# Two K^T tiles, 512-column products in three projections, and a new tile layout in a two-layer diffusion block on one core

## The chip, the cores and the metric

The kernel runs on one core of a Trainium2 chip. The metric is the device time of one execution in microseconds (us). TensorE (PE) multiplies, with its weight loads listed as PEld; VectorE is DVE, ScalarE is ACT, GpSimd is POOL and SyncE is SP. SP and POOL issue the transfers.

## The reference, cut to what matters

Two layers act on 256 tokens of width 2048; only layer 0 also carries 256 context tokens. All matrices are float32.

```python
# layer 0: gated delta rule (16 heads of 128) beside a gated short convolution
p = h @ w_in                      # for x and for ctx
q, k, v = split(silu(conv(qkv)))  # q, k normalised
o, S = _gdn_chunk_scan(f(qc), f(kc), f(vc), ...)   # context first, both directions
o, _ = _gdn_chunk_scan(f(qx), f(kx), f(vx), ..., s_ctx)
y_b = b_g * conv(c_g * h_b, w_conv_b) * silu(z_b)
x = x + gate * (concat([rmsnorm(o) * silu(z), y_b]) @ w_out)
# layer 1
u, v = split(gelu(uv))
y_c = u * (w_s @ layernorm(v) + b_s) * silu(z_c)
y_d = einsum(mean_of_neighbours(p_d) - p_d, pool_w) * pool_scale * silu(z_d)
x = x + gate * (concat([y_c, y_d]) @ w_out)
return rmsnorm(x, final_norm_w)
```

## The kernel before

Float32 accuracy comes from splitting: every weight chunk of 128x1024 values (512 KB) is loaded (`raw`), rounded to a high part `H` on ACT (line 202), and the rest `L` is formed on DVE (line 209); `wchunk` does this, with four buffers each for raw, H and L, and `extra` pools that add a buffer to every third chunk in two places. Activations are split the same way. A product is then the sum of three: H with the activation's high part, H with its low part, and L with its high part. Each product instruction loads 128x128 weights of its own.

The work stands in this order:

- The first keys and values (`wset`): for each of 16 slices of the model width, modulation, normalised transposed activations (`h_cols`, into `hxH`, `hxL`, `hcH`, `hcL`, x and context), and products of six blocks of 128 (`k_part`, line 450) that are added up in six `acc` tiles in SBUF.
- The other keys and values (`proj` on `wkv`, 10 steps; products at line 230), each 2 blocks of 128 for 256 tokens of x and 256 of context. Key rows go to memory (`ktd`, `kkd`, `vvd`) and come back by head group. The gates of the delta rule are made by `ab_rows` in step 6.
- The delta rule in four groups of four heads. A group loads K^T (`KTt`), K and V on POOL's queue, projects the queries (`wq`) and the gate (`wza`), forms Gram matrices (`G`) and masks, inverts triangular blocks (`LB`, `PT`, `XT`, `X`), and then scans eight steps (`kS`, `QS`, `z`, `Sp`, `az`), ending in a norm (`on`) and a transpose (`oT`). Between these the scheduler puts products of `wq`, `wza` and `wbb` (short convolution), 24 blocks of 192 products each.
- The output projection of layer 0, the norm and split of `h1`, and layer 1: value (`wv1`), pool branch (`wpz`, `poolw`), token mix (`wuz`), output (`wout1`).

A scheduler that simulates the program sets the order on every engine before it runs; the order is then fixed. PSUM tiles `pj` (two banks of 512 columns each) exist twice, so a projection can start only when the one before the last has been read out.

The output projections (`projT_n`) take the weights chunk as the moving side, 512 columns at a time. `proj` takes the activations as the moving side, 256 columns at a time:

```python
for i, (w, t) in enumerate(((wH, 0), (wH, 1), (wL, 0))):
    for e, a in enumerate(acts):
        PE.matmul(o[:, e * 256:(e + 1) * 256] if m > 1 else o, w, a[t][:, k, :], ...)
```

Of the kernel before, what the change touches and what calls it, by code (L numbers as in the profile page):

```python
# [17 lines left out]
P = 128  # L18
# [52 lines left out]
def layout(a):  # L71
# [44 lines left out]
    r["poolw"] = f(a["o_pool_w"][0].reshape(4, 4, P, 512).transpose(0, 2, 1, 3)).reshape(4, P, D)  # L116
# [6 lines left out]
def body(ctx: ExitStack, tc: tile.TileContext, T, dbg=None):  # L123
# [187 lines left out]
    hx_stack = ExitStack()  # L311
    hxp = pool("hx", stack=hx_stack, side="right")
    hxH = hxp.tile([P, KT, 256], F32R, name="hxH")
    hxL = hxp.tile([P, KT, 256], F32R, name="hxL")
# [50 lines left out]
    with ExitStack() as ph1:  # L365
        hcp = pool("hc", stack=ph1)
        hcH = hcp.tile([P, KT, 256], F32R, name="hcH")
        hcL = hcp.tile([P, KT, 256], F32R, name="hcL")

        accp = pool("acc", stack=ph1)  # L370
        with ExitStack() as ph0:
# [6 lines left out]
            acc = [accp.tile([P, 2, 512], F32, name="kacc", tag=f"kacc{b}") for b in range(6)]  # L378
# [39 lines left out]
            def norm_tok(s):  # L418
                for n in (2 * s, 2 * s + 1):
                    junk = accp.tile([P, 2, 512], F32, name="junk", tag="kacc5")  # L420
# [9 lines left out]
            def h_cols(j, srcs=(0, 1)):  # L430
                tr = gp.tile([P, 4, P], F32, name="trp", tag="g")
                for s in srcs:
                    aH, aL = ((hxH, hxL), (hcH, hcL))[s]
# [10 lines left out]
            def k_part(w, j, ps, first, last, srcs):  # L444
                for n in range(6):
                    wH, wL = (t[:, n * P:(n + 1) * P] for t in w)
                    for i, (w_, t) in enumerate(((wH, 0), (wH, 1), (wL, 0))):
                        for q in srcs:
                            a = ((hxH, hxL), (hcH, hcL))[q]
                            PE.matmul(ps[n][:, q * 256:(q + 1) * 256], w_, a[t][:, j, :],  # L450
                                      start=first and i == 0 and q == 0, stop=last and i == 2, skip_group_check=True)
# [33 lines left out]
            if "hT" in dbg:  # L485
                tap("hT", hcH.bitcast(F32))
# [4 lines left out]
        def row(name):  # L491
            return ap.tile([64, 512], F32, name=name)

        def ab_proj():
                nonlocal ab
                wab = ap.tile([P, KT, 64], F32, name="wab")
# [4 lines left out]
                for k in range(KT):  # L501
                    for t in range(2):
                        for e, a in enumerate(((hxH, hxL), (hcH, hcL))):
                            PE.matmul(abp[:, 256 * e:256 * e + 256], wHL[:, k, :], a[t][:, k, :],
                                      start=k == 0 and t == 0 and e == 0, stop=k == KT - 1 and t == 1,
                                      skip_group_check=True)
# [112 lines left out]
        for step, b in enumerate((12, 13, 2, 3, 6, 7, 10, 11, 14, 15)):  # L619
# [3 lines left out]
            proj(T["wkv"][b // 4, b // 2 % 2, b % 2], 256, [(hxH, hxL), (hcH, hcL)], [ps[:, 0, :], ps[:, 1, :]], 1)  # L623
# [3 lines left out]
            if step == 6:  # L627
                ab_rows()

# [43 lines left out]

    tick[0], tick[2] = RATE[1], 1
    y_stack = ExitStack()
    with ExitStack() as ph2:
# [6 lines left out]
        for grp in range(4):  # L683
            h0 = grp * 4
            hs = slice(h0, h0 + 4)
            KTt = A.tile([P, 4, 512], F32, name="KTt", tag="KTt")
# [14 lines left out]
            proj(T["wq"][grp], 512, [(hxH, hxL)], [ps[:, n, :] for n in range(4)], 2)  # L701
# [503 lines left out]
```

## Time and profile before

| | |
|---|---|
| median of 3 runs | 2149.61 us (2144.79 to 2152.18) |
| the profiled execution | 2155.28 us, its span 2153.5 us |
| PE, PEld busy | 96%, 90% |
| DVE, ACT busy | 71%, 46% |
| data moved | 446 MB, mean 207 GB/s |

A product is pipelined: it lasts 0.28 us (256 columns) but the next one starts about 0.12 us after it. So a busy share near 100% only says that PE has no gap, and the pace is read from starts: the time from the first start to the last of a run of equal instructions, divided by the steps between them.

### The profile page before, as it was taken

To read this page: it belongs to the slowest core of one execution; us is meant where nothing else is said; L and a number is where in the kernel's file an instruction comes from. 1 tells how busy PE (TensorE), PEld (TensorE's weight loads), DVE (VectorE), ACT (ScalarE), POOL (GpSimd) and SP (SyncE) were. 2 spreads that over 40 slices of the span, in tenths; PEclk is the share of its full clock that TensorE was granted. 3 is DMA by queue.
4 is the path that set the end of the run, shared out by engine and by line. 5 is a ranking of instruction groups with operands and counts; after the bars stand their busy time and mean duration, and the time that the engine had idled before them with its cause. 6 is when DMAs were issued, how large, how long until landed. Compare 5 with 4: busy or idle time off the path is not lost. (4 is left out here: it accounts for less than half of the span.)

```text
span 2153.5 us, 42176 instructions
## 1 busy us (share of the span) xinstructions
PE 2069.5 (96%) x17034; PEld 1928.5 (90%) x17034; DVE 1526.0 (71%) x2715; ACT 999.5 (46%) x1728; POOL 33.8 (2%) x51
## 2 busy tenths in 40 slices
PE   6999999999999999989999999898999999999997
PEld 4789999999989999989999878677899999998886
DVE  4447987877976898489758984788687676555554
ACT  5333365225554546445645554345454444444433
POOL 0000000000000000000000000000000000000000
PEclk9999999999999999999999999999999999999999
DMA  9777655776544775366448862797866666666664
GB/s 343 263 262 243 188 182 174 238 247 233 179 134 139 247 258 179 91 225 195 133 139 258 276 187 79 253 326 260 275 219 189 180 186 197 195 187 215 192 194 131
DMA packets 151267, 446.41 MB, mean 207 GB/s; under 512 B 16512, under 2 KB 23456, under 8 KB 150048
## 3 DMA queue, kind: packets, MB, share of 16 engines
q1 hardware_dynamic: 145936, 425.37, 61.8%
q0 software_dynamic: 5136, 18.35, 2.7%
q8 instruction: 133, 2.18, 0.4%
q14 instruction: 62, 0.51, 0.1%
HBM read 423.19 MB, written 20.46 MB: 206 GB/s over the span
## 5 line engine op out<-in xcount | busy, mean ns | idle before, releaser
L209 DVE TENSOR_TENSOR L<-raw,H 128x1024 fp32r<-128x1024 f32 (+1 forms) x554 | 667.6, 1208 | 374.8 <-ACT H L202 354.1
L202 ACT CAST H<-raw 128x1024 fp32r<-128x1024 f32 (+1 forms) x554 | 574.4, 1042 | 761.7 <-PE pj L230 419.4
L230 PE MATMUL pj<-hxH,H 128*128 128x256 f32 x1856 | 528.5, 285 | 4.2 <-DVE zb L946 4.2
L230 PE MATMUL pj<-hxH,L 128*128 128x256 f32 x1856 | 527.3, 284 | 0.0
L230 PE MATMUL pj<-hxL,H 128*128 128x256 f32 x1856 | 526.8, 284 | 0.0
L230 PEld LDWEIGHTS pj<-hxH,H 128*128 128x128 f32 x1856 | 352.4, 190 | 6.3 <-DVE zb L946 4.5
L230 PEld LDWEIGHTS pj<-hxH,L 128*128 128x128 f32 x1856 | 352.4, 190 | 2.4 <-issue 1.2
L230 PEld LDWEIGHTS pj<-hxL,H 128*128 128x128 f32 x1856 | 352.4, 190 | 1.0
L230 PE MATMUL pj<-h1H,H 128*128 128x256 f32 x1024 | 290.5, 284 | 0.0
L230 PE MATMUL pj<-h1H,L 128*128 128x256 f32 x1024 | 289.8, 283 | 0.0
L230 PE MATMUL pj<-h1L,H 128*128 128x256 f32 x1024 | 289.7, 283 | 0.0
L277 DVE SCALAR_TENSOR_TENSOR acc<-araw,cs,acc 128x512 f32<-128x512 f32 x240 | 178.9, 747 | 33.0 <-DMA araw<-in_ada 20.8
L230 PEld LDWEIGHTS pj<-h1H,H 128*128 128x128 f32 x1024 | 196.5, 192 | 0.2 <-issue 0.2
L230 PEld LDWEIGHTS pj<-h1L,H 128*128 128x128 f32 x1024 | 196.5, 192 | 0.0
L230 PEld LDWEIGHTS pj<-h1H,L 128*128 128x128 f32 x1024 | 196.5, 192 | 0.0
L230 PE MATMUL pj<-hcH,L 128*128 128x256 f32 x320 | 90.4, 283 | 0.0
L230 PE MATMUL pj<-hcH,H 128*128 128x256 f32 x320 | 90.4, 282 | 0.0
L230 PE MATMUL pj<-hcL,H 128*128 128x256 f32 x320 | 90.1, 281 | 0.0
L239 PE MATMUL pj<-H,y1H 128*128 128x512 f32 x192 | 76.0, 396 | 0.0
L241 PE MATMUL pj<-H,y1L 128*128 128x512 f32 x192 | 75.9, 396 | 0.0
L240 PE MATMUL pj<-L,y1H 128*128 128x512 f32 x192 | 75.9, 395 | 0.0
L230 PEld LDWEIGHTS pj<-hcH,L 128*128 128x128 f32 x320 | 60.1, 188 | 0.5 <-issue 0.4
(428 smaller groups left out, 3659.6 us busy)
## 6 DMA issues: line engine op xcount, KB each, us to landing
raw<-in_wbb SPq DMA_DIRECT2D x128, 512.0 KB, 3.8
raw<-in_wout SPq DMA_DIRECT2D x128, 512.0 KB, 4.0
araw<-in_ada SPq DMA_DIRECT2D x192, 256.0 KB, 4.5
raw<-in_ada SPq DMA_DIRECT2D x64, 512.0 KB, 6.5
raw<-in_wpz SPq DMA_DIRECT2D x64, 512.0 KB, 3.9
raw<-in_wuz SPq DMA_DIRECT2D x64, 512.0 KB, 3.6
raw<-in_wkv SPq DMA_DIRECT2D x40, 512.0 KB, 4.7
araw<-in_ada0g SPq DMA_DIRECT2D x64, 256.0 KB, 4.5
```

The lines of the kernel that those rows point to most:

```text
L202: S.copy(H, raw)
L209: V.tensor_tensor(L, raw, H, ALU.subtract)
L230: PE.matmul(o[:, e * 256:(e + 1) * 256] if m > 1 else o, w, a[t][:, k, :], start=st and i == 0 and e == 0, stop=sp and i == 2, skip_group_ ...
L239: PE.matmul(o, xH[:, t], H[:, kk, :], start=st, stop=False, skip_group_check=True)
L240: PE.matmul(o, xH[:, t], L[:, kk, :], start=False, stop=False, skip_group_check=True)
L241: PE.matmul(o, xL[:, t], H[:, kk, :], start=False, stop=sp, skip_group_check=True)
L277: V.scalar_tensor_tensor(aacc[u // KT], raw, cs[:, k, 0:1], aacc[u // KT], ALU.mult, ALU.add)
```

## The change

- x and context activations move into one tile `hxc`, ordered (source, part, slice, token). `proj` for keys and values, `k_part` and the gate projection multiply both sources in one 512-column product, in place of two of 256 columns.
- `hx` for the delta rule is a copy of the x half, made by ACT (eight copies of 128x1024) in steps 7 to 9, in a slot that `acc8` (the `acc` tiles, the gate weights `wab` and two rows of `ab_rows`) held before.
- In layer 1, `pair` takes the place of `proj` for `wpz`, `poolw` and `wuz`: one 512-column product of H with both parts of the activation side by side, and one 256-column product of L with the high part. The halves that belong together are in different PSUM columns: ACT copies one out and DVE adds the other (`join`, or the first operation of the pool branch). A `pair` is 2 blocks of 128 and fills a `pj` tile.
- `KTt` comes from a pool of two tiles. `yb2` and `part` reuse the slots of `hx` and `KTt`.
- The `extra` pools `xh`, `xl` go, and `dynamic_dma_scratch_size` is 2048 in place of 4096.

```diff
-        hcp = pool("hc", stack=ph1)
-        hcH = hcp.tile([P, KT, 256], F32R, name="hcH")
-        hcL = hcp.tile([P, KT, 256], F32R, name="hcL")
+        hxcp = pool("hxc", stack=ph1, side="right")
+        hxc = hxcp.tile([P, 2, 2, KT, 256], F32R, name="hxc")
...
+    def both(t, k):
+        return hxc[:, :, t, k, :]
...
-                        for e, a in enumerate(acts):
-                            PE.matmul(o[:, e * 256:(e + 1) * 256] if m > 1 else o, w, a[t][:, k, :],
-                                      start=st and i == 0 and e == 0, stop=sp and i == 2, skip_group_check=True)
+                        PE.matmul(o, w, acts(t, k),
+                                  start=st and i == 0, stop=sp and i == 2, skip_group_check=True)
...
-                wab = ap.tile([P, KT, 64], F32, name="wab")
+                wab = acc8[:, 6].rearrange("p a b -> p (a b)").rearrange("p (k c) -> p k c", k=KT)
...
             if step == 6:
                 ab_rows()
+                hx = hxp.tile([P, 2, KT, 256], F32R, name="hx", tag="hx")
+            if step > 6:
+                for t in range(2):
+                    for q in range(1 if step < 9 else 2):
+                        k4 = slice(4 * (step - 7 + q), 4 * (step - 6 + q))
+                        S.copy(hx[:, t, k4], hxc[:, 0, t, k4])
...
+    KTp = pool("ktp", 2, stack=y_stack, side="right")
...
-            KTt = A.tile([P, 4, 512], F32, name="KTt", tag="KTt")
+            KTt = KTp.tile([P, 4, 512], F32, name="KTt", tag="KTt")
...
-        xh, xl = pool("xh", 1, stack=ph3), pool("xl", 1, stack=ph3)
-        extra[0] = [(None, None, None), (None, None, None), (None, xh, xl)]
...
+    def pair(src, x, kts=KT):
+        ps = pj.tile([P, 2, 2, 256], F32, name="pj", tag="pj")
+        for c in range(kts // 4):
+            H, L = wchunk(src[:, c * 1024:(c + 1) * 1024], 4)
+            for kk in range(4):
+                k = c * 4 + kk
+                for n in range(2):
+                    w = slice(n * P, (n + 1) * P)
+                    PE.matmul(ps[:, n], H[:, kk, w], x[:, :, k, :], start=k == 0, stop=k == kts - 1,
+                              skip_group_check=True)
+                    PE.matmul(ps[:, n, 0], L[:, kk, w], x[:, 0, k, :], start=False, stop=k == kts - 1,
+                              skip_group_check=True)
+        t = Wk.tile([P, 2, 256], F32, name="jn", tag="jn")
+        S.copy(t, ps[:, :, 1])
+        return ps[:, :, 0], t
+
+    def join(ps, t):
+        V.tensor_tensor(t, t, ps, ALU.add)
+        return t
...
-        ps = pj.tile([P, 4, 256], F32, name="pj", tag="pj")
-        proj(T["poolw"][g], 512, [(dH, dL)], [ps[:, n, :] for n in range(4)], 2, kts=4)
...
+        for half in range(2):
+            t = join(*pair(T["poolw"][2 * g + half], y1[:, :, e4], 4))
+            for n in range(2):
+                m = 2 * half + n
+                V.scalar_tensor_tensor(zs[:, m, :], t[:, n, :], ps5[:, m:m + 1], zs[:, m, :], ALU.mult, ALU.mult)
...
-    for blk in range(8):
-        ps = pj.tile([P, 4, 256], F32, name="pj", tag="pj")
-        proj(T["wuz"][blk], 512, [(hH, hL)], [ps[:, n, :] for n in range(4)], 2)
+    for gi in range(16):
+        uz = join(*pair(T["wuz"][gi], h1))
```

The scheduler gives another order on the engines. On PE, the end of the second group's scan stands like this before; `pj` rows are projection products.

```order
L230 MATMUL pj<-hxH,H 128x256
L230 MATMUL pj<-hxL,H 128x256
L230 MATMUL pj<-hxH,L 128x256
L909 MATMUL az<-zs,aT 128x128 x4
L867 MATMUL kS<-St,KTt 128x128 x4
L875 MATMUL QS<-St,QT 128x128 x4
L887 MATMUL z<-r,U 128x128 x4
L909 MATMUL az<-zs,aT 128x128 x4
L926 MATMUL oT<-cst,on 128x128 x8
```

And in the changed kernel, from the last projection product ahead of that group's `oT` on; nine more rows of the scan follow these, and then `oT`.

```order
L234 MATMUL pj<-hx,L 128x256
L905 MATMUL Sp<-zk,Kt 128x128
L874 MATMUL kS<-St,KTt 128x128 x4
L882 MATMUL QS<-St,QT 128x128 x4
L905 MATMUL Sp<-zk,Kt 128x128 x3
L894 MATMUL z<-r,U 128x128 x4
L905 MATMUL Sp<-zk,Kt 128x128 x4
L916 MATMUL az<-zs,aT 128x128 x4
L874 MATMUL kS<-St,KTt 128x128 x4
L882 MATMUL QS<-St,QT 128x128 x4
L894 MATMUL z<-r,U 128x128 x4
L905 MATMUL Sp<-zk,Kt 128x128 x4
```

Projection products now end about four steps ahead of the group's end; before, they ended one step ahead. The rows of the last group's scan read alike in both kernels.

On ACT, this is the place in layer 1 (second pool group) where the changed kernel goes from the gate `z` (PSUM tile `pj_17120`) to the two halves of `poolw` (`pj_17222`, `pj_17250`); `H` rows are the weight chunks that follow.

```order
L202 CAST H_17308<-raw_17306 128x1024
L1081 COPY jn_17215<-pj_17120 128x512
L202 CAST H_17330<-raw_17328 128x1024
L1081 COPY jn_17245<-pj_17222 128x512
L1065 ACTIVATE yo_121<-jn_17215 128x512
L202 CAST H_17355<-raw_17353 128x1024
L1081 COPY jn_17276<-pj_17250 128x512
L202 CAST H_17410<-raw_17408 128x1024
```

Before, one 128x1024 operation read the gate's PSUM tile there, and the products of `poolw` filled one tile in place of two:

```order
L202 CAST H_19119<-raw_19117 128x1024
L1064 ACTIVATE yo_122<-pj_18762 128x1024
L202 CAST H_19149<-raw_19147 128x1024
L202 CAST H_19182<-raw_19180 128x1024
L345 CAST y1H_17248<-yo_122 128x1024
```

Each of the three short reads now stands behind the cast of a weight chunk whose buffer is freed by the same products.

On DVE, between the layers, these are the rows ahead of `dg`, which the transposes of `h1` wait for (`rst`, `rsy` and `rsq` are the reciprocal square root of one token block); before:

```order
L338 SCALAR_TENSOR_TENSOR rsy<-rst,rsy 128x1
L988 TENSOR_REDUCE rst_5738<-sq_5737 128x1
L277 SCALAR_TENSOR_TENSOR acc<-araw,cs,acc 128x512
L336 TENSOR_TENSOR rst<-rsy 128x1
L989 TENSOR_SCALAR rsq_5739<-rst_5738 128x1
L277 SCALAR_TENSOR_TENSOR acc<-araw,cs,acc 128x512
L337 SCALAR_TENSOR_TENSOR rst<-rst,rsq_5739 128x1
L334 TENSOR_SCALAR rsy<-rsq_5739 128x1
L338 SCALAR_TENSOR_TENSOR rst_5738<-rst,rsy 128x1
L336 TENSOR_TENSOR rst<-rsy 128x1
L1020 TENSOR_SCALAR dg<-cst,rst_5738 128x128
```

And in the changed kernel:

```order
L993 TENSOR_SCALAR rsq_4197<-rst_4196 128x1
L281 SCALAR_TENSOR_TENSOR acc<-araw,cs,acc 128x512
L341 SCALAR_TENSOR_TENSOR rsy<-rst,rsy 128x1
L337 TENSOR_SCALAR rsy<-rsq_4197 128x1
L339 TENSOR_TENSOR rst<-rsy 128x1 x2
L340 SCALAR_TENSOR_TENSOR rst<-rst,rsq_4197 128x1 x2
L341 SCALAR_TENSOR_TENSOR rsy<-rst,rsy 128x1 x2
L339 TENSOR_TENSOR rst<-rsy 128x1 x2
L340 SCALAR_TENSOR_TENSOR rst<-rst,rsq_4197 128x1 x2
L341 SCALAR_TENSOR_TENSOR rst_4196<-rst,rsy 128x1
L341 SCALAR_TENSOR_TENSOR rsy<-rst,rsy 128x1
L1022 TENSOR_SCALAR dg<-cst,rst_4196 128x128
```

The roots of both token blocks now run side by side ahead of the first `dg`: between the last update of `x1` and `dg` stand 19 such small rows in place of 9, with three `acc` rows in each kernel. And on SP the load of `wab` (512 KB) has moved to the sixteenth place from the start, ahead of the second set of `ada0` chunks.

## Rows read from the trace of the kernel before

**Rows 1.** The page: span; busy time of the engines; granted clock of PE in 40 slices of the span, in tenths of full speed.

```profile
span 2153.5 us, 42176 instructions
PE 2069.5 (96%) x17034; PEld 1928.5 (90%) x17034; DVE 1526.0 (71%) x2715; ACT 999.5 (46%) x1728; POOL 33.8 (2%) x51
PEclk9999999999999999999999999999999999999999
```

**Rows 2.** The waits of PE over the whole span: what waited, for whom, us in total, times, the longest.

```profile
PE adm L386 <- DMA raw<-in_ada: 18.4, 3, 16.5
PE oT L926 <- DVE on L923: 13.1, 2, 6.6
```

**Rows 3.** The timeline of PE, first and last row of six unbroken runs of products (start, length, instruction). The rows in each run, first and last among them: 99 and 71 (`wkv`, 250 and 400 us), 171 (`k_part`), 169 (`wpz`), 134 (`wv1`), 173 (`wout1`).

```profile
250.48 0.36 PE L230 MATMUL pj<-hxH,H 128*128 128x256 f32 x1
...
262.16 0.28 PE L230 MATMUL pj<-hxL,H 128*128 128x256 f32 x1
...
399.81 0.28 PE L230 MATMUL pj<-hcH,H 128*128 128x256 f32 x1
...
407.98 0.28 PE L230 MATMUL pj<-hcH,L 128*128 128x256 f32 x1
...
191.83 0.28 PE L450 MATMUL pj<-hcH,H 128*128 128x256 f32 x1
...
211.94 0.28 PE L450 MATMUL pj<-hcL,H 128*128 128x256 f32 x1
...
1639.80 0.28 PE L230 MATMUL pj<-h1L,H 128*128 128x256 f32 x1
...
1659.96 0.28 PE L230 MATMUL pj<-h1L,H 128*128 128x256 f32 x1
...
1519.82 0.39 PE L240 MATMUL pj<-L,h1H 128*128 128x512 f32 x1
...
1549.96 0.39 PE L241 MATMUL pj<-H,h1L 128*128 128x512 f32 x1
...
2009.68 0.40 PE L240 MATMUL pj<-L,y1H 128*128 128x512 f32 x1
...
2049.82 0.40 PE L241 MATMUL pj<-H,y1L 128*128 128x512 f32 x1
```

**Rows 4.** Groups of PE's products by line and form: count, busy us, mean ns of one.

```profile
L230 PE MATMUL pj<-hcH,H 128*128 128x256 f32 x320 | 90.4, 282 | 0.0
L450 PE MATMUL pj<-hxH,H 128*128 128x256 f32 x128 | 37.3, 295 | 0.0
L450 PE MATMUL pg<-hxH,H 128*128 128x256 f32 x64 | 18.3, 289 | 0.0
L230 PE MATMUL pj<-h1H,H 128*128 128x256 f32 x1024 | 290.5, 284 | 0.0
```

**Rows 5.** The timeline of PE at the end of the second group's scan (to 942 us) and of the fourth's: start, length, instruction, count; in brackets PE's idle time ahead of it and what ended it.

```profile
928.35 1.26 PE L887 MATMUL z<-r,U 128*128 128x128 f32 x8 [0.72 <-DVE r L870]
930.34 1.16 PE L909 MATMUL az<-zs,aT 128*128 128x128 f32 x8 [0.73 <-ACT zs L894]
938.07 1.94 PE L926 MATMUL oT<-cst,on 128*128 128x128 f32 x8 [6.57 <-DVE on L923]
...
941.38 1.79 PE L742 MATMUL G<-KTt 128*128 128x128 f32 x8
...
1332.25 1.26 PE L887 MATMUL z<-r,U 128*128 128x128 f32 x8 [0.22 <-DVE r L870]
1335.34 2.08 PE L898 MATMUL Sp<-zk,Kt 128*128 128x128 f32 x8 [1.82 <-ACT zk L891]
...
1342.25 1.26 PE L898 MATMUL Sp<-zk,Kt 128*128 128x128 f32 x8 [0.59 <-ACT zk L891]
...
1344.49 1.06 PE L867 MATMUL kS<-St,KTt 128*128 128x128 f32 x8
...
1346.28 1.06 PE L887 MATMUL z<-r,U 128*128 128x128 f32 x8
1348.07 1.16 PE L909 MATMUL az<-zs,aT 128*128 128x128 f32 x8 [0.73 <-ACT zs L894]
...
1352.63 1.16 PE L909 MATMUL az<-zs,aT 128*128 128x128 f32 x8 [0.73 <-ACT zs L894]
```

**Rows 6.** POOL's timeline at the load of K^T for the third group, and two rows of the transfers: KB each, median us from issue to landing.

```profile
927.15 0.76 POOL L692 DMA_DIRECT2D KTt<-ktd  x1 [9.11 <-PE kS L867]
...
KTt<-ktd POOLq DMA_DIRECT2D x4, 1024.0 KB, 7.1
...
wab<-in_wab SPq DMA_DIRECT2D x1, 512.0 KB, 3.7
```

**Rows 7.** Groups of ACT and DVE by line and form (the last one in the stretch 1455 to 1475 us): count, busy us, mean ns of one, idle time ahead of them.

```profile
L202 ACT CAST H<-raw 128x1024 fp32r<-128x1024 f32 x522 | 547.9, 1055 | 707.8 <-PE pj L230 419.4 <-PE pj L241 148.2 <-issue 63.6
...
L209 DVE TENSOR_TENSOR L<-raw,H 128x1024 fp32r<-128x1024 f32 x522 | 637.2, 1223 | 348.9 <-ACT H L202 330.8 <-PE kvp L599 8.9 <-PE Sp L898 2.5
...
L337 DVE SCALAR_TENSOR_TENSOR rst<-rst,rsq 128x1 f32<-128x1 f32 x5 | 0.8, 154 | 0.0
```

**Rows 8.** Two stretches by engine: us and instructions of PE, PEld, DVE, ACT and POOL, PE's granted clock, share of the DMA engines, GB/s.

```profile
0.00:54.00 54.00, 34.73 (x295) 24.15 (x296) 24.37 (x68) 28.49 (x49) 0.20 (x4) 0.97 0.93 343
1640.00:1700.00 60.00, 60.00 (x503) 60.00 (x502) 41.27 (x64) 27.26 (x34) 0.00 (x0) 1.00 0.61 182
```

More of the change, by code (lines that the diff above doesn't have):

```diff
@@ L377, in body @@
             k0r = pool("k0r", 3, stack=ph0)
-            acc = [accp.tile([P, 2, 512], F32, name="kacc", tag=f"kacc{b}") for b in range(6)]
+            acc = [acc8[:, b] for b in range(6)]
             def ada_cols(j):
@@ L432, in h_cols @@
                 for s in srcs:
-                    aH, aL = ((hxH, hxL), (hcH, hcL))[s]
+                    aH, aL = hxc[:, s, 0], hxc[:, s, 1]
                     for n in (2 * s, 2 * s + 1):
@@ L447, in k_part @@
                     for i, (w_, t) in enumerate(((wH, 0), (wH, 1), (wL, 0))):
[L448 to L451, printed above, removed]
+                        q = slice(srcs[0], srcs[-1] + 1)
+                        PE.matmul(ps[n].rearrange("p (s t) -> p s t", s=2)[:, q], w_, hxc[:, q, t, j, :],
+                                  start=first and i == 0 and srcs[0] == 0, stop=last and i == 2, skip_group_check=True)
             ssh = tp.tile([P, 4, 2], F32, name="ssh")
@@ L502, in ab_proj @@
                     for t in range(2):
[L503 to L506, printed above, removed]
+                        PE.matmul(abp.rearrange("p (s t) -> p s t", s=2), wHL[:, k, :], both(t, k),
+                                  start=k == 0 and t == 0, stop=k == KT - 1 and t == 1, skip_group_check=True)
                 ab, abl = row("ab"), row("a_")
@@ L622, in body @@
             ps = pj.tile([P, 2, 512], F32, name="pj", tag="pj")
-            proj(T["wkv"][b // 4, b // 2 % 2, b % 2], 256, [(hxH, hxL), (hcH, hcL)], [ps[:, 0, :], ps[:, 1, :]], 1)
+            proj(T["wkv"][b // 4, b // 2 % 2, b % 2], 256, both, [ps[:, n, :].rearrange("p (s t) -> p s t", s=2) for n in range(2)], 1)
             if early:
@@ L700, in body @@
             ps = pj.tile([P, 4, 256], F32, name="pj", tag="pj")
-            proj(T["wq"][grp], 512, [(hxH, hxL)], [ps[:, n, :] for n in range(4)], 2)
+            proj(T["wq"][grp], 512, one(hxH, hxL), [ps[:, n, :] for n in range(4)], 2)
             for i in range(3):
@@ L724, in body @@
             ps = pj.tile([P, 4, 256], F32, name="pj", tag="pj")
-            proj(T["wza"][grp], 512, [(hxH, hxL)], [ps[:, n, :] for n in range(4)], 2)
+            proj(T["wza"][grp], 512, one(hxH, hxL), [ps[:, n, :] for n in range(4)], 2)
             for i in range(3):
@@ L934, in body @@
                 ps = pj.tile([P, 4, 256], F32, name="pj", tag="pj")
-                proj(T["wbb"][j], 512, [(hxH, hxL)], [ps[:, n, :] for n in range(4)], 2)
+                proj(T["wbb"][j], 512, one(hxH, hxL), [ps[:, n, :] for n in range(4)], 2)
                 cg = B.tile([P, 256], F32, name="cg", tag="ct")
@@ L949, in body @@
                 dma(ydram[16 + j], yb)
[L950 to L953 removed]
+        yb2 = hxp.tile([P, 2, 16, 256], F32R, name="yb2", tag="hx")
+        ybH, ybL = yb2[:, 0], yb2[:, 1]
         def yact(k):
@@ L957, in yact @@
             return aH[:, k % 16, :], aL[:, k % 16, :]
-        partp = pool("part", stack=y_stack, side="right")
-        part = partp.tile([P, 2, 2, 512], F32, name="part")
+        part = KTp.tile([P, 2, 2, 512], F32, name="part", tag="KTt")
         def out_part(cbs, pss, order, begin=False, end=False):
@@ L992, in body @@
     H1 = pool("h1")
-    hH = H1.tile([P, KT, 256], F32R, name="h1H")
-    hL = H1.tile([P, KT, 256], F32R, name="h1L")
+    h1 = H1.tile([P, 2, KT, 256], F32R, name="h1")
+    hH, hL = h1[:, 0], h1[:, 1]
     Wo = pool("wo", 2)
@@ L1065, in silu_to @@
         V.scalar_tensor_tensor(dst, dst, 1.0, src, ALU.add, ALU.mult)
+    def pair(src, x, kts=KT):
[16 more added lines that the diff above has]
+        return t
     for g in range(4):
         r = RADII[g]
-        ps = pj.tile([P, 4, 256], F32, name="pj", tag="pj")
-        proj(T["wpz"][2 * g], 512, [(hH, hL)], [ps[:, n, :] for n in range(4)], 2)
         e4 = slice(4 * (g % 2), 4 * (g % 2) + 4)
```

94 lines of the change are left out of this document (45 added, 49 removed).

## The prediction

> **What bounds the kernel now.** I read five things, in this order: the page, PE's waits, the pace of its products from the timeline, the scan ends and POOL's queue that the change touches, and the engines that feed PE.
>
> The page says that PE is busy for 96% of 2153.5 us, with a granted clock in the upper tenth in all 40 slices [rows 1]. Clock is therefore not what can be won. The waits show how little idle time there is: 18.4 us for the first `in_ada` chunks, 13.1 us at two `oT`, and single waits below a microsecond or two [rows 2, 5]. So the time is a sum over products of their pace, and an edit counts if it changes the number of products or their pace.
>
> Lengths of single rows (0.28 and 0.39 us) overlap and are no pace. The pace is from starts [rows 3]. In `wkv`, 98 steps take 262.16 − 250.48 = 11.68 us, 119.2 ns each; later 70 steps take 8.17 us, 116.7 ns. `k_part`: 170 steps in 20.11 us, 118.3 ns. `wpz`: 168 in 20.16 us, 120.0 ns. Products of 512 columns: 133 steps in 30.14 us, 226.6 ns (`wv1`), and 172 in 40.14 us, 233.4 ns (`wout1`). For 128 columns, `kS` starts at 1344.49 and `z` at 1346.28 with 16 products between: 111.9 ns [rows 5]. Halving 256 columns to 128 thus saves 5 to 8 ns and no more: below 256 columns something that belongs to each product, such as its weight load, sets the pace, and at 256 columns the two are close. So a merge saves little: the columns stay.
>
> **What merging is worth.** The count comes first. 320 `hcH,H` products are shown [rows 4]; with `hcL,H` and `hcH,L` that is 960, each of which merges with its `hx` partner: 960 merges in `proj`. In `k_part`, 128 and 64 `H` products per source and kind are (128 + 64) × 3 = 576 pairs; slice 0 keeps its two halves apart (36 pairs), which leaves 540, and the gate projection gives 32: 572. In layer 1, 1024 `h1H,H` products [rows 4] are as many trios of three 256-column products, and `poolw` has 4 × 16 more: 1088 trios become a 512 and a 256.
>
> No row shows a 512-column product with activations in two pieces of 256 as the moving side, or a 512 and a 256 in turn. The nearest are the plain 512-column rows. I take:
>
> - `proj`: 2 × 119.2 − 233.4 = 5.0 ns × 960 = 4.8 us. Low end: 2 × 116.7 − 233.4 = 0. High end: 238.4 − 226.6 = 11.8 ns, 11.3 us.
> - `k_part` and gates: 236.6 − 233.4 = 3.2 ns × 572 = 1.8 us; low end 0; high end 10.0 ns, 5.7 us.
> - layer 1: a trio takes 3 × 120.0 = 360.0 ns. With 226.6 + 120.0 = 346.6 it saves 13.4 ns, × 1088 = 14.6 us. I use 226.6 and not 233.4, since `wv1` stands in the same layer, just ahead. Low end: 360.0 − 233.4 − 120.0 = 6.6 ns, 7.2 us. High end: if the 256-column product costs only what a 128-column one does, because its weight load hides behind 512 columns, 360.0 − 226.6 − 111.9 = 21.5 ns, 23.3 us.
>
> Sum: −21.2 us, between −7.2 and −40.3.
>
> The Trainium skill (TensorE: Matmul & The Clock Gate, Back-to-back issue gap) speaks against so much: its gap between products at the full clock is columns / 2.4 plus 2.5 ns, so a merge would save one 2.5 ns whatever the size, an estimate of 2620 × 2.5 = 6.6 us in place of 21.2. Its sustained 131 ns for 512 columns does not agree with 226.6 ns here. By the isolated formula 256 columns would take 109 ns and 512 would take 216; the rows have 117 to 120 and 227 to 233, so the fixed part here is larger, and I go by the rows.
>
> **What is added.**
>
> - *Scan end of group 2.* It loses the products that filled it. The last group's end stands without them already: its idle times are 0.22 + 1.82 + 0.59 + 0.73 + 0.73 = 4.1 us, and those of group 2 are 0.72 + 0.73 = 1.45 us [rows 5]. The difference, +2.6 us, is the price (0 if the fillers only move to a place that waits as much, 8 if three lost steps each cost as much again). The products themselves aren't lost; they run earlier.
> - *PSUM in layer 1.* A `pair` of 32 trios lasts 32 × 346.6 = 11.1 us, and reading it out is short beside that. Only `poolw` has short ones: half a `poolw` is 8 trios, 2.8 us, and the tile ahead of it must be read out in that time. That happens at the `z`-to-`poolw` and the `poolw`-to-next hand-over, 8 places. ACT's cast of a chunk stands ahead of the copy (1.055 us), the copy is half of such an operation (0.53), DVE may be in a chunk's subtraction (1.223), and the join is half of that (0.61) [rows 7]: 3.4 us at worst, 2.3 us if each is met half done. So 0 to 0.6 us × 8; I take +2 us, with 6 as the upper end.
> - *From layer 0 to layer 1.* DVE has 19 small rows ahead of `dg` in place of 9, 154 ns each [rows 7], while PE waits for the transposes: +1.5 us; 5 if some wait on each other.
> - *`wab` early.* 512 KB more [rows 6] stand in a stretch in which the DMA engines are 93% busy at 343 GB/s [rows 8], and PE waits for such loads [rows 2]: 512 KB / 343 GB/s = 1.5 us at most for one; I take +1, 3 if an `ada0` chunk is overtaken too.
> - *Copies to `hx`.* Eight of 128x1024 on ACT, 8.4 us by the cast's 1.055 [rows 7], in a row. The weight casts queue behind them, then `L` on DVE, then products. A chunk in merged `proj` is 24 products × 233.4 = 5.6 us, and up to three prepared chunks (16.8 us) lie ahead: 0. If only one were ready, 8.4 − 5.6 = 2.8 us.
> - *Copies and joins in layer 1.* In 60 us of `wpz`, DVE is busy for 41.27 and ACT for 27.26 [rows 8]. A join each 11.1 us adds 0.61 / 11.1 = 5% to DVE: hidden at 0, apart from the hand-over. The `extra` H and L buffers go; with the chunk cast and split in 2.28 us against 16 trios, 5.5 us, the four buffers left suffice. If they didn't, that stands under D.
>
> **What the two K^T tiles are worth.** Nothing. The load for the third group is issued at 927.15, after a wait of 9.11 us for `kS`, and lands 7.1 us later, at 934.3 [rows 6]. `G`, which needs it, starts at 941.38, behind `oT` of 938.07, which waits for DVE's norm, not for the load [rows 5]. The load is 7 us early already; with a tile of its own it would be earlier still. Should the landing be later than the median, the cover is these 7 us.
>
> The additions sum to 2.6 + 2 + 1.5 + 1 = +7.1 us, from 0 to about 25. With −21.2 that is −14.1 us. The profiled execution took 2155.28 us, so a like one would take 2141.2; it lies 5.7 us above the median, and in terms of the median the forecast is 2149.6 − 14.1 = 2135.5 us.
>
> **The rivals.** Changes below 0.3%, 6.4 us, are about what a measurement can't tell from none.
>
> - *A, the forecast*: 2135.5 us, between 2128 and 2143 by the size of its terms. Chance 0.48.
> - *B, weight loads were in the way*: merged products run at the best 512-column pace and the 256-column partner at 111.9 ns: −40.3 + 7.1 = −33.2, 2116.4 us. For it: PEld is 90% busy [rows 1], and 128 columns cost nearly what 256 do. Against: `wout1`, with 512 columns throughout, runs at 233.4. Chance 0.14. [...]
> - *C, a merge saves next to nothing*: columns set the pace in both forms. −7.2 + 7.1 = −0.1, 2149.5 us. For it: 2 × 116.7 is exactly 233.4 [rows 3]. Against: trios at 120.0 beside 226.6 in the same layer. Chance 0.22. The Trainium skill's isolated gap, above, would give −6.6 + 7.1 = +0.5, 2150.1 us, and is the same case.
> - *D, slower*: at the 8 short hand-overs in layer 1, the copy stands behind a cast whose H buffer is freed only by the products that wait. Each further chunk handled ahead of the copy and join costs 1.055 + 1.223 = 2.28 us. The gain without the hand-over's 2 us is 16.1; so it is spent at 16.1 / 8 = 2.0 us a place, and measurably slower from 22.5 / 8 = 2.8 us. With one chunk more than the worst case, 0.6 + 2.28 = 2.9 us a place, 23 us, 2156.5 us; with two, 5.2 a place, 41 us, 2175 us. For it: the order on ACT, with three reads of 512 columns behind casts. Against: the last 16 trios of a pair give 5.5 us to prepare chunks. Chance 0.16.
>
> That a part does nothing holds for the K^T tiles, at 0 in all cases. One term lies outside: the 128-column products of the delta rule read `hx` and K^T from other places in the schedule; a nanosecond on some 4600 would be 5 us either way, and I have no row for it.
>
> **How the numbers follow.** The likeliest case gives 2135.5. The range goes from B's 2116 less a little to D with one chunk, 2157: A and C lie in it, most of B and half of D; about 0.8 to 0.85. Faster by over 0.3%: A except its upper edge, and B, with none of C, 0.60. Within: C, A's edge and part of D, 0.27. Slower: D beyond its threshold, or C with the additions at their upper ends, 0.13.
>
> **What would show it.** In the trace after: the pace of merged `proj` should be 227 to 233 ns, and a trio in layer 1 (one 512 start to the next) 340 to 353 ns; 340 or less is B, 353 and more is C. The row `oT` of group 2 should have some 4 us of idle rows ahead of it in place of 1.45. PE's rows of 512 columns behind `poolw` should wait under a microsecond for `jn` on DVE or ACT; 2 us and more is D. `G` must not wait for K^T's load, and the waits for `in_ada` should grow by about 1 us. The forecast is wrong above all if the trio's pace is not 346.6 ns: each 10 ns there are 10.9 us.

## The result, and the profile after

The changed kernel takes 2136.66 us (median of five runs, 2131.01 to 2138.60) against 2149.54 us: a ratio of 0.9944, 95% interval 0.9929 to 0.9960; the medians are 12.9 us apart. The forecast was 14.1 us less and 2135.5 us. The sum came out; most of its terms did not, and this section shows where the time really left.

The page of the kernel after, its first lines:

```profile
span 2134.3 us, 37062 instructions
PE 2051.9 (96%) x14414; PEld 1785.0 (84%) x14414; DVE 1546.9 (72%) x2767; ACT 1024.3 (48%) x1764; POOL 34.0 (2%) x51
PEclk9999999999999999999999999999999999999999
```

2620 products are gone, as counted (17034 − 14414), and PEld is less busy than in [rows 1]. To see the time by stage I take the borders from starts on PE: the last gate product, the last key or value product, the last `oT`, the last `tr`, the last `wv1` product, the first `wout1` product. Before was profiled three times in all (the first is that of the rows ahead of the prediction, the two others are told of below); its column holds all three.

| stage (us) | before, three profiles | after | difference to the mean | forecast |
|---|---|---|---|---|
| start to the gates, with `k_part` | 226.9, 226.5, 226.8 | 225.1 | −1.6 | −0.8 |
| keys and values | 246.1, 245.9, 245.9 | 243.0 | −3.0 | −4.8 |
| delta rule | 888.9, 876.7, 884.9 | 875.8 | −7.7 | +2.6 |
| output of layer 0, `h1` | 116.5, 116.9, 116.4 | 116.4 | −0.2 | +1.5 |
| `wv1` | 84.5, 84.5, 84.5 | 84.5 | 0 | 0 |
| pool branch and token mix | 400.3, 400.3, 400.3 | 399.4 | −0.9 | −12.6 |
| `wout1` to the end | 190.3, 190.4, 190.3 | 190.1 | −0.2 | 0 |

So the stage with the largest forecast gain gained next to nothing (0.9 us), and the delta rule, from which I expected a small loss, gained most. The first came out 11.7 us worse than forecast and the second 10.3 us better; that the sum fits is luck. Both have to be explained.

**The pace is as forecast.** PE's timeline of the kernel after: first and last row of an unbroken run of merged products in `proj` (88 of them), and of a run of `pair` in layer 1 (94 steps from one 512-column product to the next). Columns: start, length, instruction.

```profile
227.23 0.39 PE L234 MATMUL pj<-hxc,L 128*128 128x512 f32 x1
...
247.61 0.40 PE L234 MATMUL pj<-hxc,L 128*128 128x512 f32 x1
...
1610.29 0.39 PE L1076 MATMUL pj<-h,H 128*128 128x512 f32 x1
...
1642.88 0.39 PE L1076 MATMUL pj<-h,H 128*128 128x512 f32 x1
```

A merged product takes 20.38 us / 87 = 234.3 ns (233.4 were taken), and a trio of layer 1 takes 32.59 us / 94 = 346.7 ns (346.6 were taken). At 360 before, 1024 trios alone should have saved 13.6 us.

**Where layer 1 lost it.** PE's timeline after, at the first `poolw` (rows left out are the products between; in brackets the idle time ahead of a row and what ended it):

```profile
1594.93 0.50 PE L1076 MATMUL pj<-y,H 128*128 128x512 f32 x1 [0.75 <-DVE jn L1085]
...
1598.88 0.68 PE L1160 MATMUL sp<-wsT,v 128*128 128x128 f32 x4 [2.29 <-DMA wsT<-in_wsT]
...
1600.46 0.63 PE L1076 MATMUL pj<-y,H 128*128 128x512 f32 x1
1600.89 0.41 PE L1078 MATMUL pj<-y,L 128*128 128x256 f32 x1
1601.10 0.63 PE L1076 MATMUL pj<-y,H 128*128 128x512 f32 x1
...
1606.60 0.80 PE L1076 MATMUL pj<-h,H 128*128 128x512 f32 x1 [2.23 <-DVE jn L1085]
```

Three waits, 5.3 us. And behind the second and the third the products are slow: from 1600.46 to 1601.10 a trio takes 640 ns, not 347. The granted clock there shows why; stretches of the same kernel (us, busy us and instructions of PE, PEld, DVE, ACT, POOL, then PE's granted clock, DMA share, GB/s):

```profile
1590.00:1598.00 8.00, 5.85 (x38) 4.92 (x36) 7.99 (x17) 2.78 (x5) 2.34 (x5) 1.00 0.84 276
1598.00:1610.00 12.00, 8.89 (x35) 7.61 (x36) 6.76 (x11) 2.96 (x4) 1.40 (x3) 0.72 0.46 146
1610.00:1650.00 40.00, 40.00 (x232) 35.28 (x232) 30.16 (x50) 19.15 (x24) 0.00 (x0) 1.00 0.58 181
```

Behind the waits PE runs for part of 12 us at the lower level, 1.2 GHz (mean 0.72). Before, no such wait stands in this stage and its clock is 1.00. DVE is busy for 7.99 of the 8 us in which this begins: the norm of `v` falls into it. ACT and DVE in the last of the three waits:

```profile
1603.64 1.05 ACT L202 CAST H<-raw 128x1024 fp32r<-128x1024 f32 x1 [8.09 <-PE pj L1076]
1604.59 0.58 ACT L1081 COPY jn<-pj 128x512 f32<-128x512 f32 x1
...
1604.72 1.22 DVE L209 TENSOR_TENSOR L<-raw,H 128x1024 fp32r<-128x1024 f32 x1 [2.67 <-ACT H L202]
1605.86 0.68 DVE L1085 TENSOR_TENSOR jn<-jn,pj 128x512 f32<-128x512 f32 x1
```

The copy stands behind a cast that had waited 8.09 us for PE to free its buffer, and the join behind the subtraction of the same chunk. For this third wait that is the mechanism of rival D, but at one place of eight. At each of the three later `poolw` PE idles for 0.15 us, between the two halves.

### The profile page after: what moved, and what is told of

Read it like the earlier page. It is cut to its first block, busy times and chain, and to the rows that moved or that the text cites. A ratio compares the mean times of both kernels' runs of the same rounds, so it can differ in the third digit from the quotient of the medians.

```text
span 2134.3 us, 37062 instructions
## 1 busy us (share of the span) xinstructions
PE 2051.9 (96%) x14414; PEld 1785.0 (84%) x14414; DVE 1546.9 (72%) x2767; ACT 1024.3 (48%) x1764; POOL 34.0 (2%) x51
## 5 line engine op out<-in xcount | busy, mean ns | idle before, releaser
L234 PE MATMUL pj<-hx,H 128*128 128x256 f32 x3072 | 562.6, 283 | 0.0
L234 PEld LDWEIGHTS pj<-hx,H 128*128 128x128 f32 x3072 | 476.1, 189 | 3.2 <-issue 0.6
L234 PE MATMUL pj<-hx,L 128*128 128x256 f32 x1536 | 434.9, 283 | 0.0
L1076 PE MATMUL pj<-h,H 128*128 128x512 f32 x1024 | 361.1, 396 | 2.2 <-DVE jn L1085 2.2
L234 PEld LDWEIGHTS pj<-hx,L 128*128 128x128 f32 x1536 | 290.3, 189 | 2.1 <-issue 1.0
L1078 PE MATMUL pj<-h,L 128*128 128x256 f32 x1024 | 287.9, 281 | 0.0
L1076 PEld LDWEIGHTS pj<-h,H 128*128 128x128 f32 x1024 | 192.7, 188 | 46.9 <-DVE jn L1085 2.5
L234 PE MATMUL pj<-hxc,H 128*128 128x512 f32 x640 | 204.9, 399 | 0.0
L281 DVE SCALAR_TENSOR_TENSOR acc<-araw,cs,acc 128x512 f32<-128x512 f32 x240 | 178.8, 745 | 25.3 <-DMA araw<-in_ada 13.7
L1078 PEld LDWEIGHTS pj<-h,L 128*128 128x128 f32 x1024 | 194.2, 190 | 0.2 <-issue 0.2
L234 PEld LDWEIGHTS pj<-hxc,H 128*128 128x128 f32 x640 | 119.5, 188 | 28.2 <-issue 0.8
L450 PEld LDWEIGHTS pj<-hxc,H 128*128 128x128 f32 x272 | 49.8, 193 | 14.4 <-issue 4.5
L387 PE MATMUL adm<-raw,cs 128*32 128x256 f32 x512 | 42.3, 407 | 16.9 <-DMA raw<-in_ada 16.9
```

What stands on the lines that cost most here:

```text
L234: PE.matmul(o, w, acts(t, k), start=st and i == 0, stop=sp and i == 2, skip_group_check=True)
L281: V.scalar_tensor_tensor(aacc[u // KT], raw, cs[:, k, 0:1], aacc[u // KT], ALU.mult, ALU.add)
L387: PE.matmul(m[32 * kk:32 * kk + 32, 0:256], cs32[:, 4 * c + kk, :], raw[:, kk * 256:(kk + 1) * 256], start=c == 0, stop=c == 3, skip_group ...
L450: PE.matmul(ps[n].rearrange("p (s t) -> p s t", s=2)[:, q], w_, hxc[:, q, t, j, :], start=first and i == 0 and srcs[0] == 0, stop=last and ...
L1076: PE.matmul(ps[:, n], H[:, kk, w], x[:, :, k, :], start=k == 0, stop=k == kts - 1, skip_group_check=True)
L1078: PE.matmul(ps[:, n, 0], L[:, kk, w], x[:, 0, k, :], start=False, stop=k == kts - 1, skip_group_check=True)
```

## The experiments

**Layer 1 as before.** `no_pair` is the changed kernel with the three 256-column products of `proj`:

```diff
-            t = join(*pair(T["poolw"][2 * g + half], y1[:, :, e4], 4))
...
+        proj(T["poolw"][g], 512, one(dH, dL), [ps[:, n, :] for n in range(4)], 2, kts=4)
...
-        uz = join(*pair(T["wuz"][gi], h1))
...
+        proj(T["wuz"][blk], 512, one(hH, hL), [ps[:, n, :] for n in range(4)], 2)
```

> The changed kernel with layer 1 as before: three 256-column products, no pair and no join; all of the rest as changed, and PE's order the same up to layer 1. In the profile after, layer 1 from wpz to wout1 took 399.2 us against 400.1 before, although a trio's pace fell from 360 to 346-347 ns there. Theory 1 (the pairs win 13 ns x 1088 = 14 us by pace and lose some 12 us of it again at the first poolw, where PE waits three times and then runs at half clock; the gain of the kernel lies ahead of layer 1): 399 to 401 us from wpz to wout1, time 2137 to 2139 us, within 2 us of the changed kernel. Rival (the pairs carry the gain, and the profile of before misleads on its layer 1): the stage 410 us or more and about 2149 us.

Measured: 2136.24 us (2133.52 to 2140.02), ratio 0.9935 [0.9921, 0.9948], and 400.4 us for the stage. Theory 1: as they stand in the change, the pairs are worth nothing.

**The pairs alone**, in the kernel before:

```diff
-    hH = H1.tile([P, KT, 256], F32R, name="h1H")
-    hL = H1.tile([P, KT, 256], F32R, name="h1L")
+    h1 = H1.tile([P, 2, KT, 256], F32R, name="h1")
...
-        proj(T["wuz"][blk], 512, [(hH, hL)], [ps[:, n, :] for n in range(4)], 2)
+        uz = join(*pair(T["wuz"][gi], h1))
```

> The kernel before with the pairs of layer 1 alone (and the smaller scratch size that they need to fit); PE's order up to layer 1 as before. Theory 1: with the waits at the first poolw as in the changed kernel the stage takes 399 us, and the time is that of before, 2147 to 2150; if those waits do not come, since the chunks and DVE stand otherwise, 388 us and 2136 to 2139. The delta rule shows 885 to 889 us if its 13 us less in the changed kernel come from the change, and anything down to 876 if they are a matter of the single execution. Rival (the pairs carry the gain): 2136 to 2138 with the waits in place.

Measured: 2145.98 us against 2149.95, ratio 0.9981 [0.9970, 0.9992], 4.1 us less. The stage takes 394.8 us: three waits come at the same places, 4.35 us in sum (1.35, 0.77, 2.23; the middle one is for DVE's `st` here), and with none of the lower clock behind them. The 12 us from the first wait on:

```profile
1609.00:1621.00 12.00, 8.36 (x47) 6.99 (x48) 9.85 (x19) 3.60 (x5) 2.80 (x6) 1.00 0.62 181
```

The stage lies between the two cases of theory 1, and the time far from the rival's 2136 to 2138. The delta rule took 883.1 us here, between the profiles of before.

**The loads of `wsT` earlier.** One of the three waits names a load, so its issue was moved up on POOL's queue:

```diff
...
+    ws_load(0)
+    ws_load(1)
     nmu = C1.tile([P, 2], F32, name="nmu")
...
-            wsT = Wk.tile([P, 2, P], F32, name="wsT", tag="wsT")
-            qdma(wsT.rearrange("p g q -> p (g q)"), T["wsT"][:, blk * 256:(blk + 1) * 256])
...
+            if blk > 1:
+                ws_load(blk)
```

> The changed kernel with the first two loads of wsT and bsb issued on POOL's queue ahead of those of lnw and lnb; PE's order the same up to the token mix. Theory 1a (the three waits at the first poolw, 0.75 + 2.29 us for the load of wsT and 2.23 us for jn on DVE, are separate causes): the 2.29 us go, the 2.23 us for jn stay or shrink, half of the half clock behind them goes: the stage 392 to 396 us, 2130 to 2134. Theory 1b (one backlog on DVE, which does the norm of v at that time, delays all three, and the load is only named): no more than 1 us, 2136 to 2138.

Measured: 2135.42 us, 1.2 us less than the changed kernel, inside both intervals (ratio 0.9935 [0.9922, 0.9947]). The wait was still there, 2.53 us: the third load must wait until the products of the first have read its buffer. POOL's timeline of this kernel:

```profile
1593.26 0.54 POOL L1127 DMA_DIRECT2D wsT<-in_wsT  x1 [4.40 <-PE sp L1168]
```

It is issued at 1593.26 and PE waits until 1598.86. In the changed kernel, too, the load that PE waits for is the third, held up by the same products:

```profile
1593.60 0.54 POOL L1154 DMA_DIRECT2D wsT<-in_wsT  x1 [4.47 <-PE sp L1160]
```

So the edit moved only loads that were early already. It did not take the wait away, and it doesn't tell 1a from 1b.

**`poolw` without a short hand-over.** Two kernels put `poolw` alone back to one tile of four blocks with 256-column products, `pool_proj_wst` with the early loads and `pool_proj` without:

```diff
-        for half in range(2):
-            t = join(*pair(T["poolw"][2 * g + half], y1[:, :, e4], 4))
...
+        ps = pj.tile([P, 4, 256], F32, name="pj", tag="pj")
+        proj(T["poolw"][g], 512, one(dH, dL), [ps[:, n, :] for n in range(4)], 2, kts=4)
```

> The same early loads, and poolw alone goes back to one tile of four blocks with 256-column products (64 trios at 360 in place of 346.6 ns: +0.9 us), so that no half poolw hands its PSUM tile over in 2.8 us. Theory 1: PE does not wait there, the clock stays, and the stage takes 400 - 1024 x 13.4 ns = 386 to 388 us; 2124 to 2127. Rival (the hand-over is not what stalls, DVE's backlog is): PE waits as long at the next place that needs DVE, 395 us or more and 2132 or more.

> The changed kernel with poolw alone as before (one tile, 256-column products), and the loads of wsT where the change has them. The early loads alone moved the time by about 1 us, since the load that is waited for became the third one, whose buffer the first token-mix products free. Theory H (the short hand-over of PSUM at poolw is the cause; the load only falls into its time): 387 to 389 us from wpz to wout1 and 2125 to 2128 us, as with the early loads. Rival W (the load of wsT is a cause of its own): the wait of 2.3 us and the half clock behind it stay, 391 to 394 us, 2129 to 2132.

Measured: 2125.83 us (2124.29 to 2126.49), ratio 0.9888 [0.9875, 0.9902], and 2124.38 us (2121.54 to 2127.54) against 2146.93, ratio 0.9895 [0.9883, 0.9908]. Both beat both kernels. The whole stage by engine (columns as above), first in before:

```profile
1563.10:1963.10 400.00, 400.00 (x3349) 399.15 (x3348) 261.66 (x391) 179.19 (x242) 11.79 (x22) 1.00 0.64 192
```

In the changed kernel:

```profile
1545.00:1944.10 399.10, 393.39 (x2261) 343.33 (x2260) 288.16 (x446) 197.13 (x272) 11.79 (x22) 0.99 0.61 192
```

In `pool_proj`, the stage and the 30 us around the first `poolw`:

```profile
1542.00:1929.60 387.60, 387.60 (x2325) 343.07 (x2324) 283.13 (x438) 193.26 (x264) 11.79 (x22) 1.00 0.61 197
...
1582.00:1612.00 30.00, 30.00 (x197) 27.24 (x196) 27.24 (x46) 14.11 (x17) 4.29 (x8) 1.00 0.74 247
```

In `pool_proj` PE has no idle time in the stage and the clock is 1.00 throughout. By the borders of the table above the stage takes 387.9 us, inside the 387 to 389 expected. The pairs are worth 400.3 − 387.9 = 12.4 us once no tile has to be handed over in 2.8 us. That is the time of theory H. But the edit changed more than the hand-over: the scheduler's order on PE changed with it. Products of the next pair now stand between two parts of the first `poolw`, and the `sp` products that need the third load of `wsT`, in the changed kernel between the halves of `poolw`, come some 200 us later:

```profile
1592.49 0.48 PE L1076 MATMUL pj<-h,H 128*128 128x512 f32 x1
...
1596.28 0.28 PE L234 MATMUL pj<-y,H 128*128 128x256 f32 x1
...
1800.80 0.60 PE L1159 MATMUL sp<-wsT,v 128*128 128x128 f32 x4
```

So it is shown that `poolw` as pairs, with the order that comes with it, costs the gain. Whether the load of `wsT` would cost something by itself is not shown: here nothing needs it at that time. DVE is still busy for 27.24 of the 30 us around that place, so a busy DVE alone does not make PE wait.

The place does not cost the same each time. Five profiles have the three waits; the loss by the clock is (1 − clock) × 12 us, over a stretch that takes in all of the lower clock:

| | stage (us) | the waits | lost by the clock |
|---|---|---|---|
| changed kernel | 399.4 | 5.3 | 3.4 |
| `wst_early` | 398.9 | 5.6 | 1.7 |
| `kv_split` (below) | 396.8 | 4.9 | 1.7 |
| `one_kt` (below) | 396.7 | 5.6 | 1.7 |
| `pair_only` | 394.8 | 4.3 | 0 |
| `pool_proj` | 387.9 | 0 | 0 |

Waits and clock together leave 1.5 to 3.7 us of the difference to `pool_proj` without a cause shown.

**The merge in keys, values and `k_part` undone**, in the changed kernel:

```diff
-                        PE.matmul(o, w, acts(t, k),
...
+                        a = acts(t, k)
+                        if acts is both:
+                            for e in range(2):
+                                PE.matmul(o[:, e], w, a[:, e],
...
-                        q = slice(srcs[0], srcs[-1] + 1)
-                        PE.matmul(ps[n].rearrange("p (s t) -> p s t", s=2)[:, q], w_, hxc[:, q, t, j, :],
...
+                        for q in srcs:
+                            PE.matmul(ps[n][:, q * 256:(q + 1) * 256], w_, hxc[:, q, t, j, :],
```

> The changed kernel with two 256-column products in place of one of 512 in the key and value projections and in k_part (the gate projection stays merged); tiles, copies and layer 1 as changed. By rows: the keys and values from the gate projection to their end 246.1 us as before in place of 243.0, the start up to there about 1 us more; the prediction had 4.8 + 1.6. Theory O (the 9 us less in the delta rule come from another order of its instructions and are not tied to one edit): the delta rule lands somewhere between 875 and 890, since its order is mixed differently here. Theory P (they come from the tiles: hx in one copied tile, K^T twice): 876 to 878. Time 2140 to 2142 by P, up to 2153 by O.

Measured: 2141.17 us, ratio 0.9970 [0.9958, 0.9982] against the changed kernel's 0.9944: 0.26%, 5.6 us. The keys and values by engine, in this kernel:

```profile
225.30:472.20 246.90, 246.14 (x2105) 243.65 (x2104) 201.11 (x420) 114.38 (x258) 0.00 (x0) 1.00 0.60 195
```

And in the changed one:

```profile
225.10:468.10 243.00, 243.00 (x1144) 195.72 (x1143) 206.60 (x430) 114.93 (x258) 0.00 (x0) 1.00 0.64 208
```

So 3.9 us by this pair of stretches. The rest of the 5.6 us is not shown to come from the edit: by the profiles the delta rule took 3.8 us more, and the pool branch and token mix 2.6 us less. The start took 225.3 us, no more than the changed kernel's 225.1 (224.9 to 226.2 in five profiles of that order), so merging in `k_part` shows no gain beyond that spread. The delta rule took 879.6 us, in the range of theory O and 1.6 us above that of theory P. With 12 us between profiles of one program (below), that rules out neither.

**One K^T tile** in place of two:

```diff
-    KTp = pool("ktp", 2, stack=y_stack, side="right")
+    KTp = pool("ktp", 1, stack=y_stack, side="right")
```

> The changed kernel with one K^T tile in place of two. PE's order is the same up to the inversion of the fourth group. The prediction priced the second tile at nothing, since the third group's load lands 7 us before its Gram products. By that: no wait at the Gram products, the delta rule 875 to 879 us, 2136 to 2138. Rival (the tile is what the delta rule gained by): 880 us or more, 2140 or more, with a wait for K^T ahead of the Gram products of groups 2 to 4.

Measured: 2139.55 us, ratio 0.9966 [0.9955, 0.9978], 0.22% or 4.7 us above the changed kernel's, with intervals that overlap. In its profile 995.9 us lie between the last key or value product and the last `tr`, 3.7 us more than in the changed kernel (`oT` no longer ends the delta rule here). The load is never late. For group 4, POOL issues it at 1108.96:

```profile
1108.96 0.75 POOL L699 DMA_DIRECT2D KTt<-ktd  x1 [10.36 <-PE kS L874]
```

And PE starts `G`, with no wait in brackets, 24 us later:

```profile
1133.49 1.16 PE L749 MATMUL G<-KTt 128*128 128x128 f32 x8
```

What is new stands in PE's waits of this kernel (us in total, times, the longest):

```profile
PE PT L818 <- DVE UT L809: 18.3, 6, 15.0
```

One of 15.0 us, at 1242 us, at the inversion of group 4, where the changed kernel's order has `yb` products between. So the rival's time came nearer than mine, but not by its wait: the tile costs nothing by its load, while the scheduler, which sets the order, fills that group differently with one. That this wait makes the difference in time is likely and not shown.

**The kernel before, profiled again**, twice, since the first profile was 5.7 us above the median:

> The kernel before, unchanged, for a second profile: the first took 2155.3 us, 5.7 above its median. If that excess lies in the delta rule, this one has 881 to 885 us there in place of 888.9, with a granted clock of 0.97 to 0.98 in place of 0.968, and everything else within 1 us.

> The kernel before, unchanged, a third profile. The first two had 888.9 and 876.7 us in the delta rule at granted clocks of 0.968 and 0.981, with the same order and waits within 3 us. If the clock alone sets where an execution lands, the delta rule is 860 us plus what the clock loses here, within 2 us.

Measured: 2142.80 and 2150.97 us, 876.7 and 884.9 us in the delta rule. The first lies below the 881 to 885 us expected; this execution was itself 4.1 us below the median of 2146.93 us. All else is within 0.4 us (table above). The delta rule by engine, before, in its three profiles one after the other:

```profile
473.00:1361.90 888.90, 845.33 (x8077) 809.53 (x8075) 679.12 (x1328) 466.57 (x891) 9.91 (x13) 0.97 0.59 186
...
472.30:1349.00 876.70, 838.00 (x8077) 802.26 (x8075) 678.27 (x1328) 466.59 (x891) 9.91 (x13) 0.98 0.59 188
...
472.70:1357.60 884.90, 844.39 (x8076) 808.32 (x8075) 678.96 (x1328) 466.51 (x891) 9.91 (x13) 0.97 0.58 187
```

In the changed kernel:

```profile
468.10:1343.90 875.80, 838.48 (x8078) 802.36 (x8077) 679.17 (x1331) 466.77 (x891) 9.93 (x13) 0.98 0.59 189
```

And in `pool_proj`, whose order is that of the changed kernel up to layer 1:

```profile
469.10:1341.00 871.90, 834.72 (x8078) 798.98 (x8077) 678.55 (x1331) 466.28 (x891) 9.93 (x13) 0.99 0.58 190
```

DVE, ACT and POOL do the same in the same time; PE's clock differs. To four places the mean clock of these stretches is 0.9677, 0.9808, 0.9716, 0.9804 and 0.9866. What the clock loses is (1 − clock) × length: 28.7, 16.8, 25.1, 17.2 and 11.7 us. Taken from the length, that leaves 860.2, 859.9, 859.8, 858.6 and 860.2 us. So the expectation for the third profile holds (860 + 25.1 = 885.1 against 884.9): the delta rule is a constant and what the clock takes, in both kernels.

The other profiles say the same. `pair_only` has the order of before up to layer 1 and took 883.1 us; `no_pair`, `wst_early` and `pool_proj_wst` have that of the changed kernel and took 878.5, 876.1 and 877.4 us. Less what the clock took, these four leave 859.3 to 861.5 us. So the order of before has 883.4 us on average in four profiles and the changed order 876.0 in five, 7.4 us apart, and the fastest of before (876.7) lies within the changed order's 871.9 to 878.5. The granted clock of all runs, profiled or not, gives less: a mean of 0.9851 over 46 runs of before, and 0.9873 over the 13 of `no_pair`, `pool_proj` and `pool_proj_wst`, which have the changed order and no wait in layer 1. That is 31.9 against 27.0 us lost in the whole execution, 4.9 us apart.

**One wait taken away in the kernel before.** In the second group, before, PE waits at 770 us for DVE's `zb`, which reads a block's PSUM tile behind two weight chunks and a transpose; the changed order has no wait there:

```diff
                 S.activation(th, ps[:, 3, :], AF.Tanh, scale=0.5)
-                V.scalar_tensor_tensor(th, th, 1.0, ps[:, 3, :], ALU.add, ALU.mult)
+                zc = B.tile([P, 256], F32, name="zc", tag="zc")
+                S.copy(zc, ps[:, 3, :])
+                V.scalar_tensor_tensor(th, th, 1.0, zc, ALU.add, ALU.mult)
```

> The kernel before, with ACT copying the last quarter of a wbb block's PSUM tile to SBUF, so that DVE's zb reads the copy and the tile comes free without DVE (and the smaller scratch size for the buffer). In three profiles of the kernel before, PE waits 2.5 to 3.4 us for zb on DVE in the second group, and in two of them 3.4 to 6.8 us at half clock lie there; in the changed kernel's order the wait is missing. Theory Z (this one hand-over is what the delta rule gained): the wait goes, the delta rule comes to 875 to 880 us and the time falls by 4 to 7 us against the kernel before. Rival (waits and half clock move on to the next short place, or the difference between the kernels is a sum of small ones): less than 2 us of it.

Measured: 2144.17 us against 2146.93, ratio 0.9981 [0.9969, 0.9993], 4.1 us less (1.5 to 6.7); the delta rule takes 877.7 us at a clock of 0.9800. PE's waits in before:

```profile
PE X L823 <- issue: 6.8, 2, 3.5
PE pj L230 <- DVE zb L946: 4.2, 2, 3.4
```

And in this kernel:

```profile
PE X L823 <- issue: 7.6, 3, 4.4
PE Sp L898 <- ACT zk L891: 4.8, 5, 2.1
```

The wait for `zb` is gone and some of it comes back at `X` and `Sp`. The 877.7 us lie within the three profiles of before (876.7 to 888.9), so only the time of the runs bears on theory Z. It is the lower end of that theory, about 4 us. The order on PE differs a little from there on, so it isn't that wait alone that was changed, and that the wait is what cost the 4 us is not shown by itself.

## Why the prediction was right in its time and wrong in its steps

- **"Clock is therefore not what can be won"** is the step that failed. The page's row of clock digits reads 9 in all slices, in both kernels, but a slice is 54 us long and a digit a tenth: the delta rule loses 17 to 29 us to the lower level under such a row. Its −7.7 us is the clock, as the constant 860 us shows; over all runs the clock gives nearer 5 us, so the one profile after was a good one. Why the changed order loses less is tried for one wait only (`zb`, about 4 us, with an order that changed too); the rest is open.
- **Trios in layer 1**: pace right to 0.1 ns, saving 12.4 us over 1024 trios where nothing waits (`pool_proj`), 13.7 by the 13.4 ns taken. The Trainium skill's rule (TensorE: Matmul & The Clock Gate, Back-to-back issue gap), 2.5 ns for each product saved, would have given 1024 × 2.5 = 2.6 us there, an estimate; the trace disagrees.
- **PSUM hand-over** was the mis-sized term: +2 us taken, with 6 as its upper end; `poolw` as pairs cost 11.5 us (399.4 against 387.9), and 8.8 to 11 in three more profiles. The worst case of a place, 0.6 us, held at the three later `poolw` (0.15 us of idle time each). It failed at the first, where DVE also does the norm of `v`: 3.0 us of waits for the join, 2.3 us for a load that the sum did not have at all, and 3.4 us by the lower clock behind them, with 2.8 us left over. My sum priced waits at their length; rival D had the order on ACT right, but at eight places, and priced no clock either.
- **`proj`**: 4.8 us forecast, 3.0 by the profiles, 3.9 by `kv_split`. By 234.3 ns and the 119.2 of [rows 3] a merge should save 4.1 ns, 3.9 us. `k_part`: 1.8 us forecast, none shown: 225.3 us with and 225.1 without the split. The start is shorter by 1.6 us in this profile, and by 1.1 on average in five of its order (225.6 against 226.7), for a reason that isn't known; it isn't the merge. The waits for `in_ada` did not grow by the 1 us priced for `wab`: 16.9 us here against the 18.4 of [rows 2].
- **Scan end of group 2**: it waits longer, as forecast, but by 1.05 us, not 2.6:

```profile
900.76 1.26 PE L905 MATMUL Sp<-zk,Kt 128*128 128x128 f32 x8 [0.52 <-ACT zk L898]
906.67 1.26 PE L905 MATMUL Sp<-zk,Kt 128*128 128x128 f32 x8 [0.52 <-ACT zk L898]
...
912.49 1.16 PE L916 MATMUL az<-zs,aT 128*128 128x128 f32 x8 [0.73 <-ACT zs L901]
...
917.05 1.16 PE L916 MATMUL az<-zs,aT 128*128 128x128 f32 x8 [0.73 <-ACT zs L901]
```

  2.50 us in the changed kernel against 1.45 in [rows 5]. The long `Sp` wait of the last group (1.82) did not come along.
- **Two K^T tiles**: no load is waited for with one or with two, as forecast. That the tile also changes the scheduler's order of the fourth group was not seen, though front and prediction both say that the scheduler sets it.
- **From layer 0 to layer 1**: +1.5 forecast; the wait ahead of `tr` grew from 7.7 to 8.5 us, and the stage as a whole didn't. The copies to `hx` cost nothing, as forecast: PE has no idle time in the keys and values after.

## What to carry to other kernels

A wait of about 2 us on the engine that bounds the kernel costs its length and can cost the clock behind it: three such waits in one place cost 0, 1.7 or 3.4 us more here. Price both, and read the clock in stretches of some ten microseconds, not in the page's digits. Where products are merged into wider PSUM tiles, look for the shortest group of products that fills a tile: the copy and join that empty it must end within that group, with the casts ahead of them in the engine's order counted. And a total that fits a forecast proves nothing: only the table by stage showed that two large terms were wrong with opposite signs. One profile of each kernel is not enough for such a table either: one stage moved by 12 us between profiles of the same program.

## What the runs showed of the hardware

One program in one order took 2142.80 to 2155.28 us in three profiles, and 12.2 of the 12.5 us between the fastest and the slowest lie in the delta rule, 876.7 against 888.9 us; its granted clock accounts for 11.9 of them. The prediction took changes below 6.4 us for what a measurement can't tell from none; in these three profiles nearly all of the spread is one stage's clock. A difference of that size between two orders of such a stage is to be read with the clock beside the time.
